# A hybrid decoder layer on one core: the first weight units, the bias rows, the chunk turns and the q/k buffers put in another order

## The chip, the cores and the metric

The kernel runs on one core of one Trainium2 chip. The metric is the device time of one execution in microseconds (us); lower is better. Engines are called as the profile calls them: PE (TensorE, matmuls and transposes), PEld (its weight loads), DVE (VectorE), ACT (ScalarE), POOL (GpSimd) and SP (SyncE, which here only issues transfers).

## The reference, cut to what matters

x is 256 × 2048 in float32, and all products are float32.

```python
x = x + 1/2 * SwiGLU_1(RMSNorm(x))            # gate, up: 2048 x 5632, down: 5632 x 2048
h = RMSNorm(x) @ W_in  -> [q | k | v | u]     # 2048 x 4096
a = DilatedWindowAttention(q, k, v)           # 8 heads x 128, QK norm, T5 bias, three dilations
s = GLU(S5(u))                                # 64 groups x 16 channels, 64 complex states each
x = x + concat(a, s) @ W_out                  # 2048 x 2048
x = x + 1/2 * SwiGLU_2(RMSNorm(x))
```

The S5 layer is a linear recurrence over the 256 positions; its coefficients come from exponentials, sines and cosines of small parameter tables.

## The kernel before

**Products.** A float32 product is made of three fast matmuls. The weight `w` is split into a rounded part `wh` (ACT, L292) and the rest `wl` (DVE, L295 and L297), the normed input into `xth` (ACT, L175) and `xtl` (DVE, L178). Then `xth·wh`, `xth·wl` and `xtl·wh` are summed in PSUM (L336, L337, L338). The two tiles of 128 positions are called t = 0, 1.

**The stream.** `run` (L257) goes over a list of passes: eleven gate/up pairs and four down passes of the first FFN, eight passes of `W_in`, the passes of `W_out` and of the GLU, and the second FFN. A pass has 512 columns of a weight; it is cut into groups of four 128-row tiles. A group (1 MB) is loaded on SP's queue into one of three `raw` buffers (`RAWB`), and is used as two units of 12 matmuls. The first groups alternate between gate and up (L259). `ahead` makes `wh` and `wl` up to three units before their use (`WB` = 4 buffers). `split` works in halves of 512 columns in the first four units.

**Side work.** Everything else is written as generators. After each unit, `step` lets each of them go on to its next `yield`, so that a `yield` puts what follows behind one more unit of matmuls, on all engines. `finish(g)` steps until g has ended, with no unit between. The side work that the change touches:

- The start. Twelve transposes of the identity (`warm_up`, L1105), the transpose of the first norm gain (L1112), four transposes of the first half of x's first quarter (L194), fourteen more warm-up transposes (`start`, L1169), then the first unit. `feed` transposes x quarter by quarter and makes `xth` and `xtl`.
- The bias rows. `other_gains` (L1115) loads gains and makes `flip`, an identity turned around, on POOL's queue. `bias_table` (L1137) loads two small tables, `rel` and `oh` (51 KB), also on POOL's queue, and multiplies them (L1146). Between the two, `ssm_prepare` has issued its loads and, at L455, the store of 0.9 MB of zeros to `k_d`.
- `ssm_prepare` (L428) makes the S5 matrices in four quarters. Each quarter multiplies powers (`powers`, three DVE operations of 512 columns, L676 to L678) into `wk`, with a `beat` (one step) behind each, and uses them in 32 small matmuls (L708).
- The turns. A finished chunk of 512 hidden columns (`sil`, after L380) has to be transposed for the down pass. `by_blocks` (L134) does that with 32 × 32 transposes on DVE (L139) into the one buffer `blocks`, a store from there to `h_d` in DRAM (SP), and four loads back. `up_done` (L376) starts such a turn per chunk; from chunk 5 on it waits until `ssm_prepare` has ended, and the pass of chunk 7 begins with `finish(mx["pre"])`.
- Queries and keys. `qk_done` puts the output of a q or k pass into the first half of `mx["qk"]`. `k_prepare` (L885) sums squares (ACT), takes the reciprocal root (DVE, L113 to L121), scales (ACT, L894) and transposes (PE, L880). `q_scale` turns the roots with a matmul (L906), `q_flip` transposes into the second half of `mx["qk"]`, and `head` (L915) makes scores, softmax and the transposed weights. Beside it the S5 recurrence runs on DVE (L795 to L797).
- The end. `final` (L419) adds the last product to x (DVE, L422) and stores it (L424), per tile t.

Of the kernel before, what the change touches and what calls it, by code (L numbers as in the profile page):

```python
# [16 lines left out]
P = 128  # L17
# [29 lines left out]
def hybrid_layer_kernel(  # L47
# [209 lines left out]
    def run(passes, extra, start):  # L257
# [9 lines left out]

        def dma():
# [3 lines left out]
            src = p.w[k0 * P:(k0 + 4) * P, p.n * 512:(p.n + 1) * 512].rearrange("(k p) n -> p k n", p=P)  # L272
            if i == 0:
                for k in range(2):
                    sync.dma_start(out=r[:, k:k + 1], in_=src[:, k:k + 1])
                extra(0)
                sync.dma_start(out=r[:, 2:4], in_=src[:, 2:4])
            else:
                sync.dma_start(out=r, in_=src)
            raws[i] = r  # L280
            st["dma"] += 1
            extra(i + 1)

        def split():
            u = st["split"]
            i, s = divmod(u, 2)
# [4 lines left out]
            for c in both if u < 4 else (slice(0, 2),):  # L291
                act.activation(out=h[:, c], in_=src[:, c], func=AF.Copy)  # L292
            if u < 4:
                for c in both:
                    vec.tensor_tensor(out=l[:, c], in0=src[:, c], in1=h[:, c].bitcast(F32), op=ALU.subtract)  # L295
            else:
                vec.tensor_tensor(out=l, in0=src, in1=h.bitcast(F32), op=ALU.subtract)  # L297
# [5 lines left out]
        def ahead(u):  # L303
            while st["dma"] < ng and st["dma"] < st["split"] // 2 + RAWB:
                dma()
            if st["split"] == 0:
                start()
            while st["split"] < 2 * ng and st["split"] <= (u + WB - 1 if u else 0):
                split()
                if st["split"] == 1:  # L310
                    start()
                while st["dma"] < ng and st["dma"] < st["split"] // 2 + RAWB:
                    dma()

        for i, (p, k0) in enumerate(groups):
            if k0 == p.ks[0]:
# [6 lines left out]
            for s in range(2):  # L323
                u = 2 * i + s
                ahead(u)
                h, l = wts.pop(u)
                order = [(kk, t) for kk in range(2) for t in range(NT)]
                if s == 1 and k0 == p.ks[-1]:
                    order = [(kk, t) for t in range(NT) for kk in range(2)]
                for kk, t in order:  # L330
                    k = k0 + 2 * s + kk
                    sh, sl = p.stat(k)
                    first = p.opens and k == p.ks[0]
                    last = p.done is not None and k == p.ks[-1] + 3
                    c = slice(t * P, (t + 1) * P)
                    pe.matmul(acc[t], sh[:, c], h[:, kk, :], start=first, stop=False)  # L336
                    pe.matmul(acc[t], sh[:, c], l[:, kk, :], start=False, stop=False)  # L337
                    pe.matmul(acc[t], sl[:, c], h[:, kk, :], start=False, stop=last)  # L338
                if s == 1 and k0 == p.ks[-1] and p.done:
                    spawn(call(p.done, acc), p.delay)  # L340
                step()


    def ffn(norm, w_gate, w_up, w_down, done, first):
# [31 lines left out]
        def up_done(c):  # L376
            def f(acc):
# [41 lines left out]
    def final(n):  # L419
        def f(acc):  # L420
            for t in range(NT):
                vec.scalar_tensor_tensor(out=res[n][:, t, :], in0=acc[t], scalar=0.5,  # L422
                                         in1=res[n][:, t, :], op0=ALU.mult, op1=ALU.add)
                (sync if n == 3 else pool).dma_start(out=out[0, t * P:(t + 1) * P, n * 512:(n + 1) * 512], in_=res[n][:, t, :])  # L424
        return f


    def ssm_prepare():  # L428
# [237 lines left out]
        for pc in range(4):  # L666
# [218 lines left out]
    def k_prepare(raw, dst):  # L885
# [9 lines left out]
        yield 2  # L895
        yield from flipped(raw, dst, ident, 1.0)

    def q_scale(n, raw):
# [5 lines left out]
        yield 2  # L904
# [5 lines left out]
    def q_flip(n, raw, dst):  # L910
        while mx["scored"] < 4 * n:
            yield
        yield from flipped(raw, dst, flip, qkg)

    def head(h):  # L915
# [3 lines left out]
        qt = mx["qk"][:, 1024:2048].rearrange("p (h s) -> p h s", h=4)[:, i, :]  # L919
# [67 lines left out]
    def mixer(norm, out_done):  # L987
# [20 lines left out]
        def qk_done(which, n):  # L1008
            def f(acc):
                assert not any(alive(mx[x]) for x in ("prep_k0", "prep_k1", "rq0", "qT0") if x in mx)  # L1010
                raw = mx["qk"][:, 0:1024].rearrange("p (t x) -> p t x", t=NT)
# [4 lines left out]
                else:  # L1016
                    dst = mx["qk"][:, 1024:2048].rearrange("p (h s) -> p h s", h=4)
# [78 lines left out]
    with tc.manual_schedule():  # L1096
# [18 lines left out]
        def other_gains():  # L1115
# [3 lines left out]
            pool.dma_start(out=grow[49:50], in_=k_norm)  # L1119
            pool.memset(flip, 0.0)  # L1120
# [13 lines left out]
            yield  # L1134
            yield from bias_table()

        def bias_table():  # L1137
            rel = small([34, NH], "rel")
            pool.memset(rel, 1.0)
            pool.dma_start(out=rel[0:32], in_=rel_bias)  # L1140
            oh = slots.tile([34, SPAN], F32, name="oh", tag="s1a")
            pool.dma_start(out=oh, in_=bias_rows)
            yield
            yield
# [106 lines left out]
```

## Time and profile before

| | us |
|---|---|
| median of three runs | 1803.52 |
| the runs | 1800.95, 1803.52, 1804.94 |
| the profiled execution | 1803.12 |
| its span in the profile | 1801.2 |
| granted TensorE clock over the span | 0.998 |

A row of a timeline gives the start, the busy time, the engine and line, the operation with output and inputs, the count of instructions merged into the row, and in brackets the idle time of the engine before it and what ended it. A row of the waits gives the engine, its line, what released it, then the sum of the waiting, the times and the longest. A row of windows gives the stretch and its length, the busy time of each engine with the count of its instructions, the granted clock of TensorE (1.00 is full speed), the share of the DMA engines and GB/s.

### The profile page before, as it was taken

The page shows a single profiled execution, that of the slowest core. Times are in us where ns is not written, and L with a number is a line of the kernel's source. Part 1 is how long each engine was busy: PE and PEld are TensorE (multiplying, and loading weights), DVE is VectorE, ACT ScalarE, POOL GpSimd, SP SyncE. Part 2 cuts the span into 40 slices and gives each one's busy share as a digit, 9 for nine tenths or more (in the row PEclk, how much of TensorE's full clock was granted, in tenths as well). Part 3 has the DMA queues.
Part 4 walks back from the last instruction along what each step waited for, and adds up shares of the span by engine and source line. Part 5 has one row for each costly group of instructions (what it writes and reads, how often), then busy time and mean ns, then how long its engine had stood idle before and what let it go on. Part 6 is the DMA issues. An engine that isn't in the chain of part 4 may idle for free.

```text
span 1801.2 us, 21490 instructions
## 1 busy us (share of the span) xinstructions
PE 1786.6 (99%) x8399; PEld 1475.0 (82%) x8399; DVE 1058.7 (59%) x1368; ACT 845.0 (47%) x1087; POOL 79.3 (4%) x151
## 2 busy tenths in 40 slices
PE   9999999999999999999999999999999999999998
PEld 7788888788888888888788888888888888888887
DVE  5688888455555455544985665555555555544443
ACT  5454444444444444447666555444444444443332
POOL 0400222100000000010000001000000000000000
PEclk9999999999999999999999999999999999999999
DMA  7867988877766676598576585777777677766652
GB/s 257 236 209 228 290 287 281 249 234 220 218 218 206 205 221 221 195 315 284 158 261 203 187 255 190 218 223 212 212 223 219 210 214 222 222 208 210 210 198 105
DMA packets 211013, 402.21 MB, mean 223 GB/s; under 512 B 9581, under 2 KB 40902, under 8 KB 209249
## 3 DMA queue, kind: packets, MB, share of 16 engines
q1 hardware_dynamic: 202672, 378.57, 65.9%
q0 software_dynamic: 6416, 19.13, 3.7%
q10 hardware_dynamic: 1824, 3.15, 0.6%
q8 instruction: 65, 1.06, 0.2%
q14 instruction: 36, 0.29, 0.0%
HBM read 370.00 MB, written 33.44 MB: 224 GB/s over the span
## 4 chain that ended last, share of the span: by engine, by line
PE 93%; DVE 4%; DMA 1%; POOL 1%; ACT 1%; issue 1%; SPq 0%; POOLq 0%; DVEq 0%; ACTq 0%
PE acc L336 30%; PE acc L338 30%; PE acc L337 30%; DVE wl L297 1%; DVE s1a L795 1%; DMA oh<-in_bias_rows_dram 0%; DVE s1a L796 0%; PE tp L336 0%; PE tp L338 0%; PE tp L337 0%; DMA h_d<-blocks 0%; ACT wh L292 0%; DVE slot L797 0%; PE tp L194 0%; PE tp L1108 0%
## 5 line engine op out<-in xcount | busy, mean ns | idle before, releaser
L297 DVE TENSOR_TENSOR wl<-raw,wh 128x1024 fp32r<-128x1024 f32 x628 | 768.6, 1226 | 682.3 <-ACT wh L292 681.9
L292 ACT ACTIVATE wh<-raw 128x1024 fp32r<-128x1024 f32 (+1 forms) x636 | 672.2, 1058 | 882.6 <-PE acc L338 859.3
L336 PE MATMUL acc<-wh,xth 128*128 128x512 f32 x1664 | 655.0, 394 | 1.4 <-ACT wh L292 1.4
L337 PE MATMUL acc<-wl,xth 128*128 128x512 f32 x1664 | 649.1, 390 | 2.7 <-DVE wl L297 2.2
L338 PE MATMUL acc<-wh,xtl 128*128 128x512 f32 x1664 | 649.2, 390 | 0.0
L337 PEld LDWEIGHTS acc<-wl,xth 128*128 128x128 f32 x1664 | 313.4, 188 | 67.5 <-DVE wl L297 2.7
L336 PEld LDWEIGHTS acc<-wh,xth 128*128 128x128 f32 x1664 | 313.2, 188 | 67.0 <-ACT wh L292 1.7
L338 PEld LDWEIGHTS acc<-wh,xtl 128*128 128x128 f32 x1664 | 313.0, 188 | 65.7
L336 PE MATMUL acc<-wh,hid 128*128 128x512 f32 x704 | 273.9, 389 | 0.0
L337 PE MATMUL acc<-wl,hid 128*128 128x512 f32 x704 | 273.9, 389 | 0.0
L338 PE MATMUL acc<-wh,hid 128*128 128x512 f32 x704 | 273.9, 389 | 0.0
L338 PEld LDWEIGHTS acc<-wh,hid 128*128 128x128 f32 x704 | 132.1, 188 | 27.5
L337 PEld LDWEIGHTS acc<-wl,hid 128*128 128x128 f32 x704 | 132.1, 188 | 27.5
L336 PEld LDWEIGHTS acc<-wh,hid 128*128 128x128 f32 x704 | 132.1, 188 | 27.4
L123 POOL TENSOR_TENSOR rs_t<-rstd 128x2 f32<-128x2 f32 x9 | 5.7, 630 | 637.9 <-DVE rstd L115 637.5
L139 DVE STREAM_TRANSPOSE blocks<-sil 128x512 f32<-128x512 f32 x44 | 28.6, 687 | 7.6 <-DMA h_d<-blocks 7.6
L424 POOL DMA_DIRECT2D out_dram<-res x6 | 3.3, 552 | 645.2 <-DVE res L422 645.1
L380 DVE SCALAR_TENSOR_TENSOR sil<-acc,rstd,sil 128x512 f32<-128x512 f32 x44 | 30.7, 740 | 0.0
L130 DVE TENSOR_TENSOR hid<-sil,hid 128x512 fp32r<-128x512 f32 x44 | 28.3, 684 | 0.0
L369 ACT ACTIVATE sil<-acc,rstd 128x512 f32<-128x512 f32 x44 | 27.5, 675 | 0.0
L129 ACT ACTIVATE hid<-sil 128x512 fp32r<-128x512 f32 x44 | 25.0, 614 | 0.0
L657 POOL DMA_DIRECT2D t_d<-k_d x32 | 18.0, 580 | 24.5 <-DMA k_d<-slot 24.2
(324 smaller groups left out, 848.7 us busy)
## 6 DMA issues: line engine op xcount, KB each, us to landing
raw<-in_ffn_w_up_dram SPq DMA_DIRECT2D x88, 1024.0 KB, 5.9
raw<-in_ffn_w_down_dram SPq DMA_DIRECT2D x88, 1024.0 KB, 5.1
raw<-in_ffn_w_gate_dram SPq DMA_DIRECT2D x87, 1024.0 KB, 5.8
raw<-in_w_in_dram SPq DMA_DIRECT2D x32, 1024.0 KB, 5.6
raw<-in_w_out_dram SPq DMA_DIRECT2D x16, 1024.0 KB, 6.0
h_d<-blocks SPq DMA_DIRECT2D x28, 512.0 KB, 7.0
sil<-h_d SPq DMA_DIRECT2D x88, 128.0 KB, 7.1
m_d<-s4b POOLq DMA_DIRECT2D x16, 256.0 KB, 4.9
```

The source lines that it names most:

```text
L129: act.activation(out=h, in_=src, func=AF.Copy)
L130: vec.tensor_tensor(out=l, in0=src, in1=h.bitcast(F32), op=ALU.subtract)
L139: vec.transpose(out=b[:, :, t].rearrange("p j (k c) -> p j k c", k=4), in_=src[:, t, :].rearrange("p (k j c) -> p j k c", k=4, j=4))
L292: act.activation(out=h[:, c], in_=src[:, c], func=AF.Copy)
L297: vec.tensor_tensor(out=l, in0=src, in1=h.bitcast(F32), op=ALU.subtract)
L336: pe.matmul(acc[t], sh[:, c], h[:, kk, :], start=first, stop=False)
L337: pe.matmul(acc[t], sh[:, c], l[:, kk, :], start=False, stop=False)
L338: pe.matmul(acc[t], sl[:, c], h[:, kk, :], start=False, stop=last)
L369: act.activation(out=sil[c][:, t, :], in_=acc[t], func=AF.Silu, scale=norm.scale(t))
L380: vec.scalar_tensor_tensor(out=a[:, t, :], in0=acc[t], scalar=norm.scale(t), in1=a[:, t, :], op0=ALU.mult, op1=ALU.mult)
L657: pool.dma_start(out=stores[0][1], in_=stores[0][2])
L795: vec.tensor_tensor(out=tm, in0=a8, in1=prev.unsqueeze(1).broadcast_to([P, 2, 2, NG]), op=ALU.mult)
```

## The change

1. The first four units are taken in the order gate k 0–1, up k 0–1, gate k 2–3, up k 2–3 (before: both gate units, then both up units), and SP's first loads follow that order: x's first half quarter, gate 0, gate 1, up 0–1, x's second half, gate 2–3, up 2–3, the second quarter of x. The first half of `wh` is rounded on ACT ahead of `xth`. In the first unit all products with `wh` come first and the four with `wl` last. The second warm-up has five transposes for fourteen.
2. `rel` and `oh` are loaded by `other_gains` ahead of `flip`, and their matmul comes one unit earlier.
3. The turn of chunk c waits for the turn of chunk c − 1 as well.
4. In `ssm_prepare`, the `wk` part of each quarter has six steps for seven.
5. k and q raws of the two halves alternate between the halves of `mx["qk"]`; `k_prepare` and `q_scale` each wait one more step ahead of their PE work, and `q_flip` waits for the keys.
6. The last tile of the output is summed in two halves of 256 columns, and the second is stored from ACT's queue.

The core of the diff:

```diff
+        units = [(0, 0), (1, 0), (0, 1), (1, 1)] + [(i, s) for i in range(2, ng) for s in range(2)]
...
+            if i == 0:
+                rs = [rawp.tile([P, 4, 512], F32, name=nm("raw"), tag="raw") for _ in range(2)]
+                for v, a, b in ((0, 0, 1), (0, 1, 2), (1, 0, 2), (0, 2, 4), (1, 2, 4)):
+                    sync.dma_start(out=rs[v][:, a:b], in_=part(*groups[v])[:, a:b])
+                    if v == 1 and a == 0:
+                        extra(0)
...
                 act.activation(out=h[:, c], in_=src[:, c], func=AF.Copy)
+                if u == 0 and c == both[0]:
+                    start()
...
+            if u == 0:
+                order = [(kk, t, v) for kk in range(2) for v in (0, 2) for t in range(NT)]
+                order += [(kk, t, 1) for kk in range(2) for t in range(NT)]
...
-                    while c >= 5 and first and alive(mx["pre"]):
+                    while (c >= 5 and first and alive(mx["pre"])) or (c and alive(turn[c - 1])):
                         yield
...
+                for c in (slice(0, 256), slice(256, 512)) if n == 3 and t == 1 else (slice(0, 512),):
+                    vec.scalar_tensor_tensor(out=res[n][:, t, c], in0=acc[t][:, c], scalar=0.5,
+                                             in1=res[n][:, t, c], op0=ALU.mult, op1=ALU.add)
+                    eng = pool if n < 3 else act if c.start else sync
...
                 powers(wk[:, :, k:k + 2, :], k, 2, cs, csw)
                 yield from beat()
-                if k != 3:
+                if k in (1, 5):
                     yield from beat()
...
-        yield 2
+        yield 3
         yield from flipped(raw, dst, ident, 1.0)
...
-        while mx["scored"] < 4 * n:
+        while alive(mx[f"prep_k{n}"]):
             yield
...
+                o = 1024 if (which == "k") == (n == 0) else 0
+                raw = mx["qk"][:, o:o + 1024].rearrange("p (t x) -> p t x", t=NT)
...
+            rel = small([34, NH], "rel")
+            pool.memset(rel, 1.0)
+            pool.dma_start(out=rel[0:32], in_=rel_bias)
+            oh = slots.tile([34, SPAN], F32, name="oh", tag="s1a")
+            pool.dma_start(out=oh, in_=bias_rows)
             pool.memset(flip, 0.0)
...
-                warm_up(14)
+                warm_up(5)
```

PE's first instructions in before (`tp` with `ident` alone is a warm-up transpose; the two `acc` are the tiles t = 0 and 1):

```order
L1112 MATMUL tp_133<-ident,grow 128x16
L194 MATMUL tp_156<-ident,res_83 128x128 x4
L1108 MATMUL tp_165<-ident 128x128 x14
L336 MATMUL acc_142<-wh_180,xth_154 128x512
L337 MATMUL acc_142<-wl_181,xth_154 128x512
L338 MATMUL acc_142<-wh_180,xtl_155 128x512
L336 MATMUL acc_143<-wh_180,xth_154 128x512
```

The same place of the changed kernel:

```order
L1127 MATMUL tp_133<-ident,grow 128x16
L194 MATMUL tp_160<-ident,res_83 128x128 x4
L1123 MATMUL tp_169<-ident 128x128 x5
L350 MATMUL acc_142<-wh_155,xth_158 128x512
L350 MATMUL acc_143<-wh_155,xth_158 128x512
L350 MATMUL acc_142<-wh_155,xtl_159 128x512
L350 MATMUL acc_143<-wh_155,xtl_159 128x512
```

The first matmul stands nine transposes earlier, and the first product with `wl` has moved from the second place to the ninth.

On DVE, at the end of the S5 preparation, the turns of chunks 5 and 6 (`blocks`) stand so in before:

```order
L297 TENSOR_TENSOR wl_2838<-raw_2744,wh_2837 128x1024
L380 SCALAR_TENSOR_TENSOR sil_555<-acc_2684,rstd_137,sil_555 128x512
L380 SCALAR_TENSOR_TENSOR sil_555<-acc_2685,rstd_137,sil_555 128x512
L139 STREAM_TRANSPOSE blocks_2862<-sil_555 128x4x128 x2
L297 TENSOR_TENSOR wl_2868<-raw_2744,wh_2867 128x1024
L139 STREAM_TRANSPOSE blocks_2887<-sil_555 128x4x128 x2
L297 TENSOR_TENSOR wl_2891<-raw_2785,wh_2890 128x1024
```

The second of the two turns in the changed kernel, where nine `wl` stand between it and the first:

```order
L311 TENSOR_TENSOR wl_2967<-raw_2862,wh_2966 128x1024
L311 TENSOR_TENSOR wl_2985<-raw_2902,wh_2984 128x1024
L130 TENSOR_TENSOR hid_2835<-sil_552,hid_2835 128x4x128 x2
L139 STREAM_TRANSPOSE blocks_3005<-sil_552 128x4x128 x2
L311 TENSOR_TENSOR wl_3011<-raw_2902,wh_3010 128x1024
```

One `wl` stood between the two turns; now the first turn's result (`hid`) is back before the second begins.

POOL's queue around the bias tables in before, from the end of the preparation's loads:

```order
L452 DMA slot_86_560<-in_ssm_d_dram 16x4x16
L454 MEMSET s2a_558 128x1792
L455 DMA k_d<-s2a_558 128x16x112
L1139 MEMSET rel_674 34x8
L1140 DMA rel_674<-in_rel_bias_dram 32x8
L1142 DMA oh<-in_bias_rows_dram 34x384
```

And in the changed kernel, right behind the loads of the gains:

```order
L1134 DMA grow<-in_k_norm_dram 1x16x8
L1136 MEMSET rel_525 34x8
L1137 DMA rel_525<-in_rel_bias_dram 32x8
L1139 DMA oh<-in_bias_rows_dram 34x384
L1140 MEMSET flip 128x128
L1141 AFFINE_SELECT flip<-flip 128x128
```

The three rows of `rel` and `oh` are moved ahead of sixteen others, the preparation's loads and the store to `k_d` among them.

More of the change, by code (lines that the diff above doesn't have):

```diff
@@ L266, in run, with part, spent @@
         st = {"dma": 0, "split": 0}
+        units = [(0, 0), (1, 0), (0, 1), (1, 1)] + [(i, s) for i in range(2, ng) for s in range(2)]
+        def part(p, k0):
+            return p.w[k0 * P:(k0 + 4) * P, p.n * 512:(p.n + 1) * 512].rearrange("(k p) n -> p k n", p=P)
+        def spent():
+            n = st["split"]
+            return n // 2 if n >= 4 else max(0, n - 2)
         def dma():
@@ L270, in dma @@
             p, k0 = groups[i]
-            r = rawp.tile([P, 4, 512], F32, name=nm("raw"), tag="raw")
[L272 to L279, printed above, removed]
+            if i == 0:
[4 more added lines that the diff above has]
+                        extra(0)
+                raws[0], raws[1] = rs
+                st["dma"] = 2
+                extra(2)
+                return
+            r = rawp.tile([P, 4, 512], F32, name=nm("raw"), tag="raw")
+            sync.dma_start(out=r, in_=part(p, k0))
             raws[i] = r
@@ L285, in split @@
             u = st["split"]
-            i, s = divmod(u, 2)
+            i, s = units[u]
             src = raws[i][:, 2 * s:2 * s + 2, :]
@@ L303, in ahead @@
         def ahead(u):
-            while st["dma"] < ng and st["dma"] < st["split"] // 2 + RAWB:
+            while st["dma"] < ng and st["dma"] < spent() + RAWB:
                 dma()
-            if st["split"] == 0:
-                start()
-            while st["split"] < 2 * ng and st["split"] <= (u + WB - 1 if u else 0):
+            while st["split"] < 2 * ng and st["split"] <= (u + WB - 1 if u else 1):
                 split()
@@ L311, in ahead @@
                     start()
-                while st["dma"] < ng and st["dma"] < st["split"] // 2 + RAWB:
+                while st["dma"] < ng and st["dma"] < spent() + RAWB:
                     dma()
-        for i, (p, k0) in enumerate(groups):
-            if k0 == p.ks[0]:
+        for u, (i, half) in enumerate(units):
+            p, k0 = groups[i]
+            if k0 == p.ks[0] and half == 0:
                 if p.pre:
@@ L322, in run @@
             acc = p.box["acc"]
[L323 to L341, printed above, removed]
+            ahead(u)
+            h, l = wts.pop(u)
+            end = half == 1 and k0 == p.ks[-1]
+            order = [(kk, t, v) for kk in range(2) for t in range(NT) for v in range(3)]
+            if u == 0:
+                order = [(kk, t, v) for kk in range(2) for v in (0, 2) for t in range(NT)]
+                order += [(kk, t, 1) for kk in range(2) for t in range(NT)]
+            elif end:
+                order = [(kk, t, v) for t in range(NT) for kk in range(2) for v in range(3)]
+            for kk, t, v in order:
+                k = k0 + 2 * half + kk
+                sh, sl = p.stat(k)
+                first = p.opens and k == p.ks[0] and v == 0
+                last = p.done is not None and k == p.ks[-1] + 3 and v == 2
+                pe.matmul(acc[t], (sh, sh, sl)[v][:, t * P:(t + 1) * P], (h, l, h)[v][:, kk, :], start=first, stop=last)
+            if end and p.done:
+                spawn(call(p.done, acc), p.delay)
+            step()
     def ffn(norm, w_gate, w_up, w_down, done, first):
@@ L1009, in f @@
             def f(acc):
-                assert not any(alive(mx[x]) for x in ("prep_k0", "prep_k1", "rq0", "qT0") if x in mx)
-                raw = mx["qk"][:, 0:1024].rearrange("p (t x) -> p t x", t=NT)
+                assert not any(alive(mx[x]) for x in ("rq0", "qT0") if x in mx) and mx["scored"] >= (4 if which == "q" and n else 0)
+                o = 1024 if (which == "k") == (n == 0) else 0
+                raw = mx["qk"][:, o:o + 1024].rearrange("p (t x) -> p t x", t=NT)
                 for t in range(NT):
@@ L1133, in other_gains @@
                                      op0=ALU.mult, op1=ALU.mult)
[L1134 to L1144, printed above, removed]
+            yield 2
             ps = tps()
```

10 lines of the change are left out of this document (4 added, 6 removed).

## The prediction, as put on record before the result was known

> **What bounds the kernel now.** I read the page first: the span, the busy times and the shares of the chain that ended last.
>
> ```profile
> span 1801.2 us, 21490 instructions
> PE 1786.6 (99%) x8399; PEld 1475.0 (82%) x8399; DVE 1058.7 (59%) x1368; ACT 845.0 (47%) x1087; POOL 79.3 (4%) x151
> PE 93%; DVE 4%; DMA 1%; POOL 1%; ACT 1%; issue 1%; SPq 0%; POOLq 0%; DVEq 0%; ACTq 0%
> ```
>
> TensorE (PE) is busy for 1786.6 of 1801.2 us, and the chain of waits runs over it for 93%. The change takes no product away, so it can only win what PE loses: the time in which it waits, and the time in which it runs slowly. The view of waits, for PE alone, names the first kind.
>
> ```profile
> PE tp L1146 <- DMA oh<-in_bias_rows_dram: 2.3, 1, 2.3
> PE acc L337 <- DVE wl L297: 2.2, 1, 2.2
> PE acc L336 <- ACT wh L292: 1.4, 1, 1.4
> ...
> PE tp L880 <- ACT s4a L894: 1.1, 2, 0.8
> PE tp L880 <- ACT s5a L958: 0.6, 1, 0.6
> PE acc L337 <- DVE wl L295: 0.5, 1, 0.5
> PE tp L906 <- DVE qk_rs L121: 0.4, 1, 0.4
> ```
>
> That is 8.5 us in eight waits. The second kind is in the view of windows (length, busy time of PE, PEld, DVE, ACT and POOL with counts, then the granted clock).
>
> ```profile
> 7.10:10.50 3.40, 3.40 (x19) 2.81 (x18) 1.35 (x3) 0.28 (x1) 0.00 (x0) 1.00 1.04 400
> 10.50:13.90 3.40, 1.46 (x7) 0.84 (x6) 1.85 (x4) 2.72 (x6) 0.00 (x0) 1.00 1.04 386
> 13.90:17.30 3.40, 3.40 (x9) 2.63 (x8) 2.76 (x6) 2.29 (x4) 0.00 (x0) 0.50 0.70 195
> 72.00:75.40 3.40, 1.73 (x10) 1.07 (x10) 3.16 (x10) 0.44 (x1) 0.00 (x0) 1.00 0.58 139
> 75.40:78.80 3.40, 3.40 (x9) 2.73 (x9) 3.33 (x8) 1.07 (x1) 1.56 (x3) 0.50 0.83 274
> 78.80:82.20 3.40, 3.40 (x16) 2.78 (x16) 2.19 (x7) 1.06 (x1) 0.00 (x0) 1.00 0.75 189
> 348.40:351.80 3.40, 3.04 (x13) 2.54 (x14) 3.40 (x4) 0.21 (x1) 0.00 (x0) 1.00 0.65 188
> ```
>
> Twice a stretch in which PE was busy for about half (1.46 and 1.73 of 3.40) is followed by one at clock 0.50. The second of these holds 9 matmuls where the next one, at 1.00, holds 16: a half-clock stretch loses 7 matmuls. Behind the wait of 2.2 for wl, which ended at 348.8, the clock stayed at 1.00 (last row), so a wait doesn't always bring one.
>
> **The start.** Weights come in groups, each rounded by ACT (wh), subtracted by DVE (wl) and multiplied in two units of 12 matmuls.
>
> ```profile
> 4.35 1.11 PE L194 MATMUL tp<-ident,res 128*128 128x128 f32 x4
> 5.26 2.60 PE L1108 MATMUL tp<-ident 128*128 128x128 f32 x14
> 5.50 0.84 ACT L175 ACTIVATE xth<-tp,gain_f 128x256 fp32r<-128x256 f32 x2 [2.75 <-PE tp L194]
> 6.23 1.15 ACT L292 ACTIVATE wh<-raw 128x512 fp32r<-128x512 f32 x2
> 7.61 0.47 PE L336 MATMUL acc<-wh,xth 128*128 128x512 f32 x1
> 10.55 0.60 PE L194 MATMUL tp<-ident,res 128*128 128x128 f32 x4
> 17.18 1.22 DVE L297 TENSOR_TENSOR wl<-raw,wh 128x1024 fp32r<-128x1024 f32 x1 [0.64 <-ACT wh L292]
> 20.55 1.03 PE L194 MATMUL tp<-ident,res 128*128 128x128 f32 x8
> 24.16 0.39 PE L336 MATMUL acc<-wh,xth 128*128 128x512 f32 x1
> 24.84 0.39 PE L336 MATMUL acc<-wh,xth 128*128 128x512 f32 x1
> ```
>
> The fifth unit starts at 24.16 in before. Three matmuls take 24.84 − 24.16 = 0.68, so one takes 0.227 and a unit 2.72. After the change: nine transposes fewer stand before the first matmul. Five take about 1.25 (0.28 each as the four at 4.35, 0.19 as the mean of the fourteen), so the first matmul can start at 5.26 + 1.25 = 6.5. ACT has wh's first half done before the transposes end (it is free until 5.50), and xth by 6.34. Then four units of 2.72 (10.9), the four transposes of x's second half and the eight of the next quarter (0.45 + 0.87, the rows above without their ramp) give 18.75. I add 0.25 for a start of which part may be at half clock, and 0.6 for xtl and wl, which DVE makes one behind the other: 19.6. Gain 24.16 − 19.6 = **4.5** (rounded down). It can be checked: waits 1.4 + 0.5, one half-clock stretch 7 × 0.227 = 1.6, and 1.1 from the shorter warm-up are 4.6. What covers it: the second gate/up weight halves arrive behind one more 0.5 MB; at 400 GB/s (window 7.10) that is 1.3 us more, and x's second half, needed after the first unit at 9.2, came early enough for its transposes at 10.55 in before without a wait. If it is late by up to 1.4, that 1.4 and a half-clock stretch (1.6) are lost: lower bound 1.5. Upper bound 4.9 (no wait for xtl). The fifth unit's wl ends at 18.4 in before (17.18 + 1.22), its load has the same bytes ahead, so it is no new bound.
>
> **The bias rows.** Four rows of the timeline:
>
> ```profile
> 56.30 0.53 POOL L447 DMA_DIRECT2D s2b<-in_ssm_b_im_dram  x1
> 62.50 1.17 POOL L455 DMA_DIRECT2D k_d<-s2a  x1 [0.30 <-POOL s2a L454]
> 64.61 0.56 POOL L1142 DMA_DIRECT2D oh<-in_bias_rows_dram  x1
> 73.67 0.80 PE L1146 MATMUL tp<-oh,rel 34*8 34x384 f32 x2 [2.32 <-DMA oh<-in_bias_rows_dram]
> ```
>
> The load of oh was issued at 64.61, behind the 0.9 MB store at 62.50 on GpSimd's (POOL's) queue, and PE waited until 73.67 for it: 9.1 from issue. It is now issued ahead of flip's memset and of the preparation's loads, of which one stands at 56.30: over 8 us earlier, and ahead of that store, while its matmul comes one unit (2.72) earlier. Even with 9.1 us again it would land by 56.3 + 9.1 = 65.4, and the matmul, ready at 73.67 − 2.32 = 71.35 in before, is due at 68.6: the wait goes. With it goes the half-clock stretch (1.6), and 0.35 of slow restart (two matmuls of 384 columns took 0.80 where 2 × 0.17 = 0.34 is their share of 0.227 per 512): 2.3 + 1.6 + 0.4 = **4.3**. Bounds 2.3 (a half-clock stretch comes anyway) to 4.7. Cost: the memset of rel and the two issues, which filled POOL from 62.50 + 1.17 to 64.61 + 0.56, push the preparation's loads back by 1.5. The one at 56.30, with 9.1 us for its landing as well, comes at 66.9; its transposes stand right behind the bias matmul's new place, at 68.6: 0, and up to 1 if it takes longer than oh did.
>
> **The turns.** Chunk 5 and 6 were both held until the S5 preparation ended, and then turned at once through one buffer.
>
> ```profile
> 346.30 1.30 DVE L139 STREAM_TRANSPOSE blocks<-sil 128x512 f32<-128x512 f32 x2 [7.60 <-DMA h_d<-blocks]
> 347.53 4.59 DVE L297 TENSOR_TENSOR wl<-raw,wh 128x1024 fp32r<-128x1024 f32 x4
> ```
>
> DVE stood 7.60 us until the first store had read the buffer, with four wl of 1.15 behind it, and PE waited 2.2 for the first. Now turn 6 starts only when turn 5 has ended; its transposes meet an empty buffer, and only its generator waits, no engine. Gain 2.2 + 0.2 restart = **2.4**, bounds 1.0 (the later turn 6 costs PE a shorter wait at another wl) to 2.5.
>
> **The attention heads.** The keys' and queries' transposes come one unit later each, so ACT's scaled rows are there. Four waits of 1.1 + 0.6 + 0.4 = 2.1, with four slow restarts at most 3.2. But DVE is nearly full here:
>
> ```profile
> 887.90:897.40 9.50, 8.08 (x40) 6.07 (x38) 8.68 (x33) 7.44 (x17) 0.00 (x0) 1.00 0.43 123
> 897.40:920.00 22.60, 21.94 (x104) 18.04 (x105) 21.34 (x54) 15.96 (x35) 0.00 (x0) 1.00 0.57 186
> ```
>
> DVE works 8.68 + 21.34 = 30.02 of these 32.10 us, and the change takes none of it away. So PE can shorten them by 2.08 before it waits for wl instead: **2.0**, bounds 0 and 3.2.
>
> **Shorter beats in the S5 preparation.** Each quarter loses one step, so that its PE work comes one unit earlier behind DVE's powers.
>
> ```profile
> 179.05 0.69 DVE L678 TENSOR_TENSOR slot<-slot,tp 128x512 f32<-128x512 f32 x1
> 183.54 1.08 PE L708 MATMUL tp<-slot,s2a 128*32 128x128 f32 x32
> ```
>
> The powers end at 179.74, and PE uses them at 183.54: 3.80 of slack, of which 2.72 goes, 1.1 stays. Cost **0**; if DVE comes later by one more wl (1.22) in each quarter, 4 × 0.1 plus at most one half-clock stretch: 2. A gain is excluded, since PE did not wait there.
>
> **The tail.** The last tile's sum and store:
>
> ```profile
> 1795.18 0.69 DVE L422 SCALAR_TENSOR_TENSOR res<-acc,res 128x512 f32<-128x512 f32 x1 [7.20 <-PE acc L338]
> 1795.91 1.72 SPq L424 DMA_DIRECT2D out_dram<-res  x2
> 1796.55 0.69 DVE L422 SCALAR_TENSOR_TENSOR res<-acc,res 128x512 f32<-128x512 f32 x1 [0.67 <-PE acc L338]
> ```
>
> Two halves take about 0.42 each (0.69 for 512 columns, 0.42 an estimate from half of it and a fixed part), so the second half's store is issued 0.15 later, the first 0.27 earlier, and each moves half of the bytes, on two queues: **0.1**, bounds −0.3 to 0.4.
>
> The sum: 4.5 + 4.3 + 2.4 + 2.0 + 0 + 0.1 = 13.3. The profiled execution took 1803.1 us, 1.9 more than its span and 0.4 less than the median 1803.5, so the forecast is 1803.1 − 13.3 = 1789.8, given as 1790.
>
> **The skill against the trace.** The windows show two half-clock stretches behind waits of 1.9 and 2.3 us. The Trainium skill, "TensorE: Matmul & The Clock Gate", section "Why this matters for your kernels", asks for no idle gap over about 3 us, and says that one idle window brings the half clock; by it neither wait would have, and the sum would be 2 × 1.6 = 3.2 smaller, 10.1. The measured rows decide: the clock was 0.50 behind both.
>
> **The rivals.**
> First, DVE takes the place of the waits at the heads. For it: the two windows above, 91% and 94% busy; against it: wl is made up to three units ahead. Then the heads' 2.0 is lost, and one more us where DVE's work is moved: gain 10.3, 1793. Chance 0.18.
>
> Second, the clock at the start. With five transposes for fourteen, PE may not have been busy enough by 7.1, and runs its first matmuls at half clock up to 10.5: one stretch, 1.6, at most two: gain 11.7 to 10.1, 1791.5 to 1793. Against it: the window from 7.10 had clock 1.00 with nothing but transposes ahead of it. The Trainium skill, same page, section "Part 4: PE-mode transpose", says that the full clock doesn't engage for transposes, as they don't count as busy in the same way; by it before, too, would have started at half clock, which the row at 7.10 contradicts. Chance 0.10.
>
> Third, slower: the shorter beats. PE waits w for the powers in each of the four quarters, and each wait brings a half-clock stretch: 4 × (w + 1.6). The gain is used up at w = 1.7, which needs DVE 2.8 later than in before (1.1 of slack first), that is two more wl or one block of powers (3 × 0.69) and a part of a wl. At w = 2.6 the price is 16.8, which gives 1807, slower by 0.2%. For it: DVE's order there is given by which steps fall together; against it: the 3.80 of slack at the quarter shown. Chance 0.05 for slower, and 0.07 for the same mechanism with w between about 0.9 and 2.6, which leaves the time within 0.2%.
>
> **How the numbers follow.** A difference under 0.2% (3.6 us) can't be told from none here. The forecast has 0.60, the rivals 0.18, 0.10, 0.07 and 0.05: faster 0.88, same 0.07, slower 0.05. All the upper bounds add up to 15.7, 1787.4; the runs scatter by 1.4 to 2.6 around their median, so the range begins at 1786. Upwards it takes in both first rivals (1793) and a start or bias term at its lower bound beside one of them (3 or 2 more), with scatter 1797.
>
> **What would show it.** In the profile of the changed kernel: the fifth unit's first matmul near 19.6; no window at clock 0.50 behind the bias matmul, which has no wait for oh; DVE's blocks without a wait near 340; PE's waits in 880 to 910 for wl alone, under 1; none at the S5 matmuls. The forecast is wrong if a half-clock stretch stands at the start, if PE waits at the S5 matmuls, or if the heads' waits come back as waits for wl.

## The result and the profile after

The changed kernel takes 1790.99 us in the median (1790.84 to 1791.75, four runs), before 1803.26 (1800.95 to 1804.94, four runs). The ratio is 0.9934 with a 95% interval of 0.9916 to 0.9951: faster by 12.3 us, where 13.3 were forecast and 1790 was the number given. The profiled execution is the slowest of the four, 1791.75 with a span of 1789.9, so against the profiled execution of before (span 1801.2) the two traces differ by 11.3.

First the page of the changed kernel, its span, busy times and the chain's shares:

```profile
span 1789.9 us, 21483 instructions
PE 1781.8 (100%) x8390; PEld 1471.1 (82%) x8390; DVE 1058.8 (59%) x1369; ACT 845.5 (47%) x1087; POOL 79.4 (4%) x151
PE 96%; DVE 2%; ACT 1%; DMA 1%; issue 0%; SPq 0%; DVEq 0%; ACTq 0%
```

Then PE's waits, all that are left:

```profile
PE tp L1123 <- POOL ident masks.py:199: 1.4, 1, 1.4
PE tp L194 <- DMA res<-in_x_dram: 1.0, 1, 1.0
PE acc L350 <- DVE wl L311: 0.8, 1, 0.8
PE acc L350 <- DVE xtl L178: 0.3, 1, 0.3
PE tp L970 <- ACT s5a L965: 0.3, 1, 0.3
```

Of the eight waits of before, all are gone; the first row stood in before too, ahead of the first instruction. In their place there are four smaller ones, 2.4 us in all.

Where the 11.3 came from is read by numbering the matmuls of 512 columns, 7584 in both kernels, twelve to a unit, and subtracting the start of each in the changed kernel from the start of the same one in before:

| place | before | changed | ahead by | gained here |
|---|---|---|---|---|
| first matmul | 7.61 | 6.17 | 1.44 | |
| fifth unit | 24.16 | 20.03 | 4.13 | |
| seventh unit | 29.60 | 26.07 | 3.53 | start: 3.5 |
| 23rd unit, after the bias matmul | 82.57 | 75.09 | 7.47 | bias rows: 3.95 |
| 109th unit, after the S5 preparation | 324.38 | 316.90 | 7.48 | beats: 0 |
| 119th unit, after the turns | 354.11 | 344.10 | 10.00 | turns: 2.5 |
| 333rd unit, after the heads | 976.00 | 965.14 | 10.87 | heads: 0.9 |
| last matmul | 1796.12 | 1785.25 | 10.87 | |
| end of the span | 1801.2 | 1789.9 | 11.3 | tail: 0.4 |

**The start** in the changed kernel's timeline for PE:

```profile
5.24 1.27 PE L1123 MATMUL tp<-ident 128*128 128x128 f32 x5
6.17 0.81 PE L350 MATMUL acc<-wh,xth 128*128 128x512 f32 x2
10.45 0.63 PE L194 MATMUL tp<-ident,res 128*128 128x128 f32 x4 [0.99 <-DMA res<-in_x_dram]
20.03 0.39 PE L350 MATMUL acc<-wh,xth 128*128 128x512 f32 x1
```

Five transposes took 1.27 (1.25 were summed) and the first product came at 6.17 (6.5). Then PE waited 0.99 for x's second half, which now stands behind one more load. No half-clock stretch follows it; the granted clock was 1.00 from 6.40 to the last matmul.

**The bias rows**, from POOL's and PE's timelines:

```profile
50.86 0.54 POOL L1139 DMA_DIRECT2D oh<-in_bias_rows_dram  x1
63.75 0.81 PE L1156 MATMUL tp<-oh,rel 34*8 34x384 f32 x2
```

No wait stands at the matmul: oh was issued 12.9 us ahead of its use. It landed in 2.1 us (the page of DMA issues for this window), for 8.9 behind the store of zeros in before. The matmuls take 0.81 here as well, so the 0.35 that the prediction took for a slow restart there wasn't one.

**The turns**, on DVE, where the second turn stood 7.60 us in before:

```profile
349.26 1.29 DVE L130 TENSOR_TENSOR hid<-sil,hid 128x512 fp32r<-128x512 f32 x2
350.46 1.30 DVE L139 STREAM_TRANSPOSE blocks<-sil 128x512 f32<-128x512 f32 x2
```

The first turn's result (`hid`) is made first, and the transposes of the second follow it without a wait. PE has no wait there.

**The heads**, in windows that take them from their first steps on:

```profile
847.00:859.00 12.00, 12.00 (x55) 9.94 (x54) 11.18 (x33) 4.31 (x5) 0.00 (x0) 1.00 0.52 161
859.00:878.00 19.00, 19.00 (x89) 15.88 (x88) 17.93 (x50) 14.40 (x39) 1.61 (x3) 1.00 0.51 153
878.00:888.00 10.00, 8.81 (x43) 6.71 (x42) 9.20 (x35) 7.25 (x20) 0.54 (x1) 1.00 0.37 117
888.00:910.00 22.00, 22.00 (x106) 18.05 (x106) 20.74 (x53) 17.07 (x37) 0.00 (x0) 1.00 0.57 188
```

DVE's busy share (third pair) is 92 to 94% in all of them, and what DVE did ahead of PE's one wait for wl is this:

```profile
879.11 0.18 DVE L113 TENSOR_SCALAR rs_ms<-qk_ss 128x8 f32<-128x8 f32 x1
881.36 0.17 DVE L121 SCALAR_TENSOR_TENSOR qk_rs<-rs_t,qk_rs 128x8 f32<-128x8 f32 x1
881.44 1.22 DVE L311 TENSOR_TENSOR wl<-raw,wh 128x1024 fp32r<-128x1024 f32 x1
```

From its first to its last row the reciprocal root holds DVE for 2.3 us, with wl behind it, and PE goes on at 882.72. Then DVE's late rows reach PE a second time, by way of ACT:

```profile
885.32 0.40 ACT L965 ACTIVATE s5a<-s5a,stat 128x128 f32<-128x128 f32 x1 [0.36 <-DVE stat L963]
885.78 0.84 PE L970 MATMUL tp<-flip,s5a 128*128 128x128 f32 x3 [0.27 <-ACT s5a L965]
```

**The tail**:

```profile
1785.67 0.76 DVE L435 SCALAR_TENSOR_TENSOR res<-acc,res 128x256 f32<-128x256 f32 x2 [0.67 <-PE acc L350]
1786.46 0.36 ACTq L438 DMA_DIRECT2D out_dram<-res  x1
```

Two halves took 0.76 together (0.42 and 0.41, overlapping), against 0.69 for the whole in before. From the last matmul's start to the end of the span it was 5.07 and is 4.68.

### The profile page after: what moved, and what is told of

Its sections match the earlier page's. It is cut to its first block, busy times and chain, and to the rows that moved or that the text cites. A ratio compares the mean times of both kernels' runs of the same rounds, so it can differ in the third digit from the quotient of the medians.

```text
span 1789.9 us, 21483 instructions
## 1 busy us (share of the span) xinstructions
PE 1781.8 (100%) x8390; PEld 1471.1 (82%) x8390; DVE 1058.8 (59%) x1369; ACT 845.5 (47%) x1087; POOL 79.4 (4%) x151
## 4 chain that ended last, share of the span: by engine, by line
PE 96%; DVE 2%; ACT 1%; DMA 1%; issue 0%; SPq 0%; DVEq 0%; ACTq 0%
PE acc L350 92%; PE tp L350 1%; DMA raw<-in_ffn_w_gate_dram 1%; DVE wl L311 1%; DVE s1a L809 0%; ACT wh L304 0%; PE tp L820 0%; DVE s1a L810 0%; PE tp L722 0%; PE tp L785 0%; ACT tp L884 0%; PE tp L995 0%; PE tp L823 0%; PE tp L194 0%; DVE slot L811 0%
## 5 line engine op out<-in xcount | busy, mean ns | idle before, releaser
L350 PE MATMUL acc<-wh,hid 128*128 128x512 f32 x1408 | 434.0, 389 | 0.0
L350 PE MATMUL acc<-wh,s4b 128*128 128x512 f32 x64 | 20.8, 394 | 0.0
L350 PE MATMUL acc<-wh,s2a 128*128 128x512 f32 x64 | 20.8, 393 | 0.0
L350 PE MATMUL acc<-wh,slot 128*128 128x512 f32 x64 | 20.7, 393 | 0.0
```

What stands on the lines that cost most here:

```text
L350: pe.matmul(acc[t], (sh, sh, sl)[v][:, t * P:(t + 1) * P], (h, l, h)[v][:, kk, :], start=first, stop=last)
```

## The experiments

All kernels are edits of the changed kernel; times are compared with its 1790.99. Each was timed in five rounds beside before, whose runs lay between 1800.2 and 1806.4 in all of them, the lowest of each session between 1800.2 and 1801.0. The runs of one kernel are spread over 0.8 us or more, so a difference of 0.6 or 0.8 between two medians is at the edge of what they can tell; the offsets between two traces are surer there.

**The old start.** The function `run` and `start` of before in the changed kernel:

```diff
-                warm_up(5)
+                warm_up(14)
...
-        units = [(0, 0), (1, 0), (0, 1), (1, 1)] + [(i, s) for i in range(2, ng) for s in range(2)]
-        for u, (i, half) in enumerate(units):
+        for i, (p, k0) in enumerate(groups):
```

> The changed kernel (1791.0 us) with the old start: unit order, first loads, first roundings and fourteen warm-up transposes as before. The offsets between the matmuls of the two traces give the start 3.5 us. If the parts add up, this kernel takes 1794.5, its first products wait 1.4 and 0.5 us for wh and wl again, and one stretch of 3.4 us at clock 0.50 follows. Rival: that stretch hangs on where a free-running clock window falls and not on the waits; then it may be missing, and the kernel takes 1792.9 (1.6 less). A time under 1792 would say that the old start costs nothing and the gain came from elsewhere.

It took 1794.05 (1793.79 to 1795.53), ratio to before 0.9959 (0.9946 to 0.9971). Two rows of its waits:

```profile
PE acc L336 <- ACT wh L292: 1.4, 1, 1.4
PE acc L337 <- DVE wl L295: 1.0, 2, 0.5
```

The waits are back as expected, 1.4 and 0.5 twice, but the profiled run has no half-clock stretch, as the rival had it:

```profile
8.57:11.99 3.42, 2.48 (x13) 1.81 (x12) 0.04 (x1) 0.91 (x3) 0.00 (x0) 1.00 1.05 402
11.99:15.40 3.41, 2.42 (x9) 1.80 (x10) 3.41 (x7) 3.05 (x6) 0.00 (x0) 1.00 0.77 258
15.40:18.81 3.41, 3.41 (x16) 2.77 (x15) 3.13 (x4) 2.01 (x2) 0.00 (x0) 1.00 0.92 330
```

The edges here are those of the granted clock's own records. The waits fall into two of these stretches, 2.48 and 2.42 busy, and the clock stays. In before they fell into one, 1.46 busy, and the clock halved. The five runs part in the same way: three with a mean clock of 1.000 took 1793.8 to 1794.1, two with 0.999 took 1795.1 and 1795.5. So the old start costs 3.0 without a half-clock stretch and about 4.3 with one. The time expected without one, 1792.9, was too low by 1: it starts from the 3.5 of the offsets, in which the changed kernel's wait of 0.99 for x is already taken off.

**The old bias rows.**

```diff
-            rel = small([34, NH], "rel")
-            pool.memset(rel, 1.0)
-            pool.dma_start(out=rel[0:32], in_=rel_bias)
-            oh = slots.tile([34, SPAN], F32, name="oh", tag="s1a")
-            pool.dma_start(out=oh, in_=bias_rows)
             pool.memset(flip, 0.0)
...
-            yield 2
+            yield
+            yield from bias_table()
```

> The changed kernel with the loads of rel and oh and their matmul at the old place. The offsets give this part 3.95 us, of which 2.3 are the wait for oh and about 1.6 a half-clock stretch. If the wait brings the stretch, this kernel takes 1795.0 and shows both. Rival: the stretch is a matter of the phase at which the wait falls (here the place comes 3.5 us earlier than in before, one clock window of 3.41 and 0.1); then it is missing and the kernel takes 1793.4. Rival two: the wait is due to the store of zeros alone, which stands ahead of oh here too, so both agree on a wait of 2.3, plus or minus 0.5.

It took 1795.09 (1794.53 to 1795.67), ratio 0.9963 (0.995 to 0.9977): 4.1 more. PE waited 2.0 for oh, and the stretch behind it is there:

```profile
67.88:71.29 3.41, 2.21 (x12) 1.49 (x13) 3.17 (x11) 0.63 (x2) 0.00 (x0) 1.00 0.53 145
71.29:74.71 3.42, 3.42 (x10) 2.67 (x9) 3.35 (x9) 0.71 (x1) 1.55 (x3) 0.50 0.76 235
```

All five runs have a mean clock of 0.999 or 0.998. The wait and a half-clock stretch of 1.6 make 3.6 of the 4.1; by the offsets of the two traces this part costs 3.7.

**The old keys and queries.**

```diff
-        yield 3
+        yield 2
         yield from flipped(raw, dst, ident, 1.0)
...
-        while alive(mx[f"prep_k{n}"]):
+        while mx["scored"] < 4 * n:
...
-                o = 1024 if (which == "k") == (n == 0) else 0
-                raw = mx["qk"][:, o:o + 1024].rearrange("p (t x) -> p t x", t=NT)
+                raw = mx["qk"][:, 0:1024].rearrange("p (t x) -> p t x", t=NT)
```

> The changed kernel with keys and queries as before (the raws in one half, two steps for three, the old wait of the flipped queries). If the new order was worth what the prediction said (2.0 us), this kernel takes 1793.0 and PE waits 2.1 us for ACT and DVE between 875 and 910. If DVE bounds that stretch, as the offsets say (0.9), it takes 1791.9, and the wait of 0.84 for wl in the changed kernel is replaced by those waits for ACT.

It took 1791.6 (1791.07 to 1792.21), ratio 0.9943 (0.993 to 0.9955): 0.6 more. The waits for ACT are those of before:

```profile
PE tp L894 <- ACT s4a L908: 1.1, 2, 0.8
PE tp L894 <- ACT s5a L972: 0.6, 1, 0.6
PE tp L920 <- DVE qk_rs L121: 0.4, 1, 0.4
```

2.1 us of waits are back, and 0.6 is the loss (0.8 by the offsets between this trace and the changed kernel's): what the change takes away there, it pays back for the most part elsewhere in the same stretch.

**The old turns with the old beats.**

```diff
-                    while (c >= 5 and first and alive(mx["pre"])) or (c and alive(turn[c - 1])):
+                    while c >= 5 and first and alive(mx["pre"]):
...
-                if k in (1, 5):
+                if k != 3:
```

> The changed kernel without the chain of the turns and with the old, longer beats in the S5 preparation. Both theories expect the old order on DVE (the second turn one wl behind the first), a wait of DVE for the buffer of some 7.6 us, PE waiting 2.2 us for wl, and 1793.5 (2.5 more). They differ in the S5 matmuls: if the shorter beats cost something (the offsets show 0 net per quarter), the kernel is less than 2.5 slower. No half-clock stretch is expected behind that wait, as before had none there.

It took 1794.73 (1793.41 to 1796.21), ratio 0.996 (0.9948 to 0.9972): 3.7 more. DVE waits for the buffer and PE for wl, as expected, but this time a half-clock stretch follows (DVE's row, then two windows at the edges of the clock's records):

```profile
338.09 1.30 DVE L139 STREAM_TRANSPOSE blocks<-sil 128x512 f32<-128x512 f32 x2 [7.66 <-DMA h_d<-blocks]
```

```profile
338.27:341.68 3.41, 1.13 (x5) 0.95 (x6) 3.41 (x5) 0.86 (x1) 0.00 (x0) 1.00 0.39 136
341.68:345.10 3.42, 3.42 (x10) 2.65 (x9) 2.22 (x2) 0.38 (x1) 0.00 (x0) 0.50 0.76 193
```

The expectation that none would come here was wrong. Two runs with a mean clock of 1.000 took 1793.4 and 1794.2, three with 0.999 took 1794.7 to 1796.2: the same part costs 2.4 to 3.2 or 3.7 to 5.2.

**The chain of turns alone** (the beats as in before):

```diff
-                if k in (1, 5):
+                if k != 3:
```

> The changed kernel with the old beats and the new chain of the turns. The prediction put the gain at the turns down to the chain and gave the beats nothing. Without the chain but with the new beats, DVE's order has five wl between the two turns in place of nine, so the beats alone would part them as well. If the chain is enough, this kernel takes 1791.0 and DVE has no wait over 2 us for the buffer; if the shorter beats are needed too, PE waits for wl at about 340 again and it takes 1792.5 to 1794.7.

It took 1790.6 (1790.29 to 1791.35), ratio 0.9928 (0.9916 to 0.9941): no more than the changed kernel. The chain alone makes the whole gain at the turns, and the shorter beats add nothing. Whether the beats alone would do as well was not tried on the chip.

**A lighter recurrence.** The second product of each step is not added, so this kernel leaves a part of the recurrence out:

```diff
-            vec.tensor_tensor(out=ts, in0=tm[:, :, 0, :], in1=tm[:, :, 1, :], op=ALU.add)
-            vec.tensor_tensor(out=cur, in0=cur, in1=ts, op=ALU.add)
+            vec.tensor_tensor(out=cur, in0=cur, in1=tm[:, :, 0, :], op=ALU.add)
```

> The changed kernel without one of the three DVE operations of every step of the S5 recurrence (the second product of the complex multiplication is not added; 0.33 us less of DVE per step). Theory: DVE is full between 847 and 890 and bounds the heads; then the wait of 0.84 for wl falls away with its restart, and the kernel takes 1790.0 against about 1791.0. Rival: the wait for wl comes from the place of the roots ahead of that wl in DVE's queue and not from the load as a whole, which would leave it at 0.5 or more and the time at 1790.7 or above; the wait of 0.27 for ACT stays in both.

It took 1789.21 (1788.78 to 1789.6), ratio 0.9927 (0.9914 to 0.9939): 1.8 less. No wait is left at the heads; behind the wait ahead of the first instruction, these are all:

```profile
PE tp L194 <- DMA res<-in_x_dram: 0.7, 1, 0.7
PE acc L350 <- DVE xtl L178: 0.3, 1, 0.3
```

```profile
859.00:878.00 19.00, 19.00 (x90) 15.83 (x89) 15.72 (x48) 15.66 (x44) 2.15 (x4) 1.00 0.57 161
878.00:888.00 10.00, 10.00 (x54) 8.34 (x53) 8.97 (x27) 8.27 (x20) 0.00 (x0) 1.00 0.41 137
```

With DVE at 15.72 for 17.93 in the second window, PE is busy through all of them. Here even the wait for ACT went, more than either theory had said. The offsets put 2.1 us into two units, the 311th and the 312th, which took 5.41 and 3.70 us in the changed kernel and 3.52 and 3.53 here. That is about twice the 0.84 and 0.27 of the named waits: PE's time around a wait, and between transposes that come one by one, is not in a wait's row. DVE's load is what keeps the heads from giving more.

**The roots on POOL** (the queries' root likewise):

```diff
-        rsqrt_(rs, ss, 8, 1.0 / HD)
-        yield
+        rsqrt_(rs, ss, 8, 1.0 / HD, pool)
+        yield 2
...
-        yield 3
+        yield 2
```

> The changed kernel with the reciprocal roots of keys and queries computed on POOL (twelve small operations of some 0.27 us by the rows of POOL for the norm, 3.3 us, beside 1.9 us that DVE saves each time), and one of the steps between the scaled keys and their transposes put ahead of the scaling. Theory (DVE bounds the heads): no wait for wl, 1790.0. Rival: the later roots make ACT wait in front of the scaling, with wh queued behind it, and PE waits for wh or for the scaled keys: 1791.5 or more.

It took 1796.44 (1794.3 to 1796.72), ratio 0.9964 (0.9951 to 0.9978): 5.4 more. Two runs with a mean clock of 1.000 took 1794.3 and 1794.8, three with 0.999 took 1796.4 to 1796.7.

```profile
PE tp L920 <- POOL qk_rs L126: 3.0, 1, 3.0
PE tp L894 <- ACT s4a L908: 1.4, 2, 0.8
```

The roots came too late for the matmul that turns them, and with two steps for three behind the scaling the waits for the scaled keys are back. It says that the roots on POOL are late, not what DVE's relief is worth.

**The keys' roots one step later** (on top of the chain alone):

```diff
-        yield
+        yield 2
         rsqrt_(rs, ss, 8, 1.0 / HD)
...
-        yield 3
+        yield 2
```

> The changed kernel with the old beats (the chain alone, 1790.6) and the keys' reciprocal roots one step later, with one step less behind their scaling, so that the wl for which PE waited stands ahead of the roots in DVE's queue. DVE's work is the same. If the wait of 0.6 to 0.9 was a matter of that one place, it goes and the kernel takes 1789.7 to 1790.1. If DVE is behind as a whole, the next wl is late instead, by 0.5 or more, or the scaled keys are (one step less for ACT), and it takes 1790.5 or more.

It took 1792.28 (1791.8 to 1793.29), ratio 0.994 (0.9926 to 0.9954), 1.7 more than the chain alone. The wait for wl is gone, and two rows show what came for it:

```profile
PE tp L894 <- ACT s4a L908: 1.6, 2, 0.8
...
PE tp L894 <- ACT s5a L972: 0.5, 1, 0.5
```

ACT's rows are late again (1.6 + 0.5 us): it needs the third step between the scaling and the transposes: that is the step which the change added.

**The whole recurrence on POOL.**

```diff
-            vec.tensor_tensor(out=tm, in0=a8, in1=prev.unsqueeze(1).broadcast_to([P, 2, 2, NG]), op=ALU.mult)
+            pool.tensor_tensor(out=tm, in0=a8, in1=prev.unsqueeze(1).broadcast_to([P, 2, 2, NG]), op=ALU.mult)
```

(the two additions likewise)

> The changed kernel with all three operations of every step of the S5 recurrence on POOL, which between 847 and 914 us issues five loads and does nothing else. It takes 30 us of work from DVE there and leaves the computation whole. If DVE's load bounds the heads, PE's wait of 0.84 for wl goes and the kernel takes 1789.0 to 1789.4, as without one of the three operations. Rival: a step takes POOL longer than the units leave it (1.8 us a step on average at 1.5 steps to a unit of 2.72), the recurrence ends later than 914 and the work on y behind it stops PE: 1792 or more. Or POOL's operations slow DVE's down beside them, and wl takes over 1.3 us for 1.22.

It took 1803.2 (1802.56 to 1804.61), ratio 1.0002 (0.9993 to 1.0011): the whole gain is gone. One row, then the groups of the lines between 850 and 905:

```profile
925.41 0.72 PE L820 MATMUL tp<-s2a,slot 128*32 128x128 f32 x8 [12.73 <-POOL slot L811]
```

```profile
L311 DVE TENSOR_TENSOR wl<-raw,wh 128x1024 fp32r<-128x1024 f32 x17 | 23.7, 1405 | 14.2 <-ACT wh L304 14.1
L809 POOL TENSOR_TENSOR s1a<-a,slot 128x256 f32<-128x256 f32 x20 | 19.3, 967 | 1.3
L811 POOL TENSOR_TENSOR slot<-slot,s1a 128x128 f32<-128x128 f32 x20 | 16.6, 829 | 1.6
```

A step took POOL 2.4 us on average (967 + 645 + 829 ns) for the 1.0 of DVE, and PE waited 12.73 for the end. At the heads, PE had no wait for wl, and there, up to the 319th unit, this trace is 1.8 us ahead of the changed kernel's. Here the recurrence is whole, so it shows what DVE's relief is worth at the heads without leaving anything out.

**Every third step on POOL.**

```diff
+            eng = pool if 8 <= m < 26 and m % 3 == 0 else vec
```

> The changed kernel with every third step of the recurrence on POOL (six steps of thirty, among those that fall beside the heads). DVE loses 6 x 1.0 us of work. By DVE's load this is enough for a wait of 0.84: 1789.5 to 1790.2. Rival: each change of the engine inside the chain of steps makes DVE wait for POOL with wl queued behind, which gives the time back: 1791 or more.

It took 1794.66 (1793.94 to 1794.85), ratio 0.9949 (0.9937 to 0.9962), 3.7 more: PE waited 3.3 for wl, with a half-clock stretch behind it. DVE waited for POOL inside the chain of steps (0.90 us at 872.09, for one), with wl behind.

**Fourteen warm-up transposes again** (`warm_up(5)` to `warm_up(14)`):

> The changed kernel with fourteen transposes in the second warm-up again. The clock was 1.00 from 6.4 us on with five, so the rival of the prediction (a half-clock start with five) expects a gain of up to 1.6 here and is already at odds with the trace. If the warm-up only delays, the first matmul comes at about 7.2 to 7.6 for 6.2 and the kernel takes 1791.5 to 1792.2; if what follows waits for the loads anyway, the delay is absorbed and it takes 1791.0.

It took 1791.69 (1791.1 to 1792.25), ratio 0.994 (0.9927 to 0.9952). The first matmul came at 6.78 for 6.17, and the median is 0.7 higher, though the runs overlap.

**One warm-up transpose in all** (`warm_up(12)` to `warm_up(1)`, `warm_up(5)` to `warm_up(0)`):

> The changed kernel with one warm-up transpose in all (for twelve and five). PE then does four transposes of x and the first matmuls in a clock window that began idle. If the full clock needs one window of steady work, and the transposes counted as such, it now comes one window later: up to 3.4 us at half clock in the first unit, 1792.0 to 1792.8. If the transposes never counted and the matmuls alone bring the clock, nothing changes but the start: 1790.5 to 1791.0.

It took 1791.81 (1791.62 to 1792.43), ratio 0.9941 (0.9929 to 0.9954): 0.8 more. Its windows at the clock's edges:

```profile
5.25:8.67 3.42, 2.85 (x7) 2.09 (x8) 2.08 (x4) 1.40 (x4) 0.00 (x0) 1.00 0.85 250
8.67:12.08 3.41, 3.41 (x12) 2.72 (x11) 1.29 (x2) 1.15 (x2) 0.00 (x0) 1.00 1.04 394
12.08:15.49 3.41, 3.41 (x17) 2.77 (x17) 2.39 (x5) 2.92 (x6) 0.00 (x0) 1.00 0.73 274
```

The clock column has no record ahead of 12.08 and shows 1.00 there for want of one; the counts tell more. The matmuls started 0.427 apart from 6.4 to 12.3, at half clock, and 0.227 after that. The full clock came only behind the stretch in which PE was busy throughout; 2.85 of 3.42 had not been enough. In the changed kernel the stretch from 2.99 to 6.40, almost all of it transposes, was followed by 0.227. So transposes do count, and the warm-up is worth 0.8. Twelve matmuls at 0.427 for 0.227 are 2.4 us, three times that; that the rest is time in which PE would have waited for its loads anyway is likely and not shown. The time lies between the two that were expected.

## Why the prediction was right, point by point

**What bounds the kernel: right.** But for the 0.4 of the tail, PE's losses were the whole gain; its busy time fell by 4.8 us and the rest was waiting.

**The start, 4.5: right in what it is, and it was sized by one state of the clock.** The trace of before had a half-clock stretch there, and with one the part is worth 4.3; without, 3.0. The 3.5 of the two profiled executions is low for another reason: the wait of 0.99 for x's second half, which the sum put at nothing and named as a load that may come too late. In the traces of the nine later kernels with this same start it is 0 in five (old bias rows and chain alone among them) and 0.2, 0.3, 0.5 and 0.7 in the others. It is a matter of when the load lands, and that profile had it late.

**The bias rows, 4.3: right.** 3.95 by the offsets and 4.1 by undoing it. The 0.35 for a slow restart was not there, since the matmuls take 0.8 without a wait. How much of it is the store to `k_d` and how much the sixteen instructions ahead as a whole was not tried apart.

**The turns, 2.4: right, for the reason given.** 2.5 by the offsets, and the chain alone makes it. The half-clock stretch that didn't follow in before can follow: then the part is worth up to 5.2.

**The heads, 2.0: wrong, by more than half.** This is the step that failed. 0.9 by the offsets, 0.6 by undoing it. The sum let PE shorten the stretch by all of DVE's 2.08 idle us. But in before's records the 2.08 are 61 pauses of under 0.1 us each between DVE's operations, which this change does not fill; whether another order would was not tried. In the changed kernel DVE shows 92 to 94% in every window and no wait by name between 876 and 890, so it was full at that. The first rival, DVE in the place of ACT, is what happened, at less than its price: one wait of 0.84 for wl behind the roots, and a wait for ACT rows that DVE's made late. So one of the prediction's own signs of being wrong was met, waits coming back as a wait for wl. The lighter recurrence shows the cause, since taking work from DVE, and from DVE alone, brought 1.8 more, and the whole recurrence on POOL was 1.8 ahead at the heads as well. Set against the lighter recurrence, before lost 2.9 us at the heads, of which the change had 0.9 back.

**Shorter beats, 0: right.** No wait stands at the S5 matmuls, and the kernel with the old beats takes 1790.6. The rival on the slower side did not occur.

**The tail, 0.1: too small.** 0.4; the halves took the 0.42 that was estimated but overlapped, so the last store was issued 0.07 later for 0.15, and, with 128 KB for 256 KB, it landed 2.13 us after its issue for 2.46.

**The second rival, a half-clock start: did not occur.** With five transposes the clock was full from 6.40, and fourteen cost 0.7 more than five in the median.

**The total.** 3.5 + 3.95 + 2.5 + 0.9 + 0.4 = 11.3 between the two profiles. The forecast of 13.3 was 2.0 too high there, by 1.0 at the start, 1.1 at the heads and 0.3 at the bias rows, less 0.4 at the turns and the tail. That the medians differ by 12.3 and come so near to 1790 is in part luck: the profiled execution of the changed kernel was its slowest.

**The Trainium skill's rule on the clock.** The Trainium skill, "TensorE: Matmul & The Clock Gate", section "Why this matters for your kernels", asks for no idle gaps of over about 3 us and gives one idle window as what brings the half clock; here waits of 2.0 (old bias rows) and 2.3 (old turns) brought one and the wait of 3.0 with the roots on POOL brought none, and the measurement decides. Its section "What's actually happening" in Part 1, where the window is 3413 ns long and free-running, agrees with the records: 3.41 us, or a multiple of it, between the edges in every kernel, at another place in each trace.

## What to carry to other kernels

Where one engine is busy 99% of the time, list its waits one by one and ask of each what is late next; a stall on a single-buffered tile or behind a big store on the same queue can be had back whole, but a wait in a stretch where another engine is over 90% busy can come back, as here, under that engine's name. Count short pauses between small instructions as work until an order is found that fills them: 94% busy was full here. A short wait may cost its length or its length and 1.6 us more, by where it falls in the clock's window, so size such a term with both, and expect the spread of the runs to shrink when the waits go.

## What was not expected of the hardware

**A half-clock stretch hangs on more than the length of a wait.** Behind the same wait it came in some runs and not in others, which points at the place of the wait in the clock's 3.41 us windows. The turns' wait of 2.23 us in before crossed an edge of them at 348.43, and no stretch followed; with the old turns the wait of 2.29 lay inside one window, and one did. But the waits for oh crossed an edge too (71.96 in before, 67.88 with the old bias rows) and were followed by one. The busy time of PE in the 3.41 us window ahead of it was 1.13 (old turns), 1.46 and 1.73 (before) and 2.21 (old bias rows); 2.42 and 2.48 (old start) brought none. Two rows do not fit, one of before and one of the kernel with the roots on POOL:

```profile
345.00:348.40 3.40, 1.53 (x7) 0.94 (x5) 2.10 (x3) 1.06 (x1) 0.00 (x0) 1.00 0.14 48
```

```profile
906.46:909.87 3.41, 1.55 (x7) 0.94 (x5) 3.24 (x9) 1.06 (x1) 2.76 (x8) 1.00 0.31 114
```

1.53 and 1.55 busy, at the edges of a window to within 0.04 us, and the clock stayed. So PE's busy time alone does not decide it. These two windows hold no transposes. Counted without transposes, PE was busy for 0.80 and 1.03 (before), 1.13 (old turns) and 1.26 (old bias rows) ahead of a stretch, which puts these two above all four; but windows with 1.19 (roots on POOL, from 882.57) and 1.26 (old start, from 5.16) kept the clock too. What decides stays open. Stretches that come and go also fit the spread of the times: before's runs lie between 1800.2 and 1806.4 with mean clocks of 0.996 to 0.999, the 11 above 1804 all at 0.997; the changed kernel's four lie within 0.9 us at 1.000.

**POOL and DVE slow each other.** With the recurrence on POOL, wl took 1405 ns for 1221 and POOL's own operation of 256 columns 967 on average for 725 at its shortest. In the kernel with every third step on POOL single DVE operations of 0.25 took up to 1.08 beside it:

```profile
878.84 1.08 DVE L957 TENSOR_SCALAR stat<-stat 128x2 f32<-128x2 f32 x1
879.13 0.75 POOL L810 TENSOR_TENSOR s1a<-a,slot 128x256 f32<-128x256 f32 x1
```

That it is the two engines' access to memory was not tested.
